# Rotating 96 planes by a quarter turn: two groups of four slabs in place of one, with two quarters laid out in rows by ScalarE

## The chip, the cores and the metric

One Trainium2 chip, one core. The metric is the device time of one launch in microseconds (us), a median over runs. Of the engines, VectorE (DVE in the profile) does the transposes, ScalarE (ACT) does plain copies, SyncE (SP) issues every DMA. TensorE does nothing; GpSimd (POOL) sets four constants at the start.

## The reference

```python
# x: float32, 32 x 3 x 256 x 256
return np.rot90(x, k=-1, axes=(-2, -1)).astype(np.float32)
```

Each of the 96 planes of 256 x 256 floats is turned clockwise: element (h, w) goes to row w, column 255 - h. No arithmetic is done. 25.17 MB are read and 25.17 MB written.

## The kernel before

**Slabs and groups.** A slab is 128 x 16 rows of 256 floats: 2 MB, or 4096 floats (16 KB) on each of the 128 partitions. There are 12 slabs, and all of them stay in SBUF at once, in five tiles `u0` to `u4` of `sizes = (2, 2, 2, 4, 2)` slabs. Each group is turned in place, so the store of a group reads the tile that its load filled.

**Loads.** A partition gets runs of neighbouring rows, and the length of one run is the length of one DMA row: 8 KB in group 0 (lines 55 and 56), 16 KB in the groups of two slabs and 32 KB in the group of four (line 66). SP issues all loads in order, group by group, 2 MB or 1 MB each; the very last 2 MB are split in two halves of 1 MB (lines 63 and 64), the first of which is called `mark`.

**Turning.** VectorE's transpose works on blocks of 32 x 32: it swaps 32 partitions with 32 elements of its free axis. Which 32 elements form a block is chosen by the access pattern, so one transpose instruction over 128 x 2048 elements moves a quarter of two slabs. The 16 rows x 16 columns of small blocks on a partition are cut in four quarters by the low and high half of the column index c and of the row index r. The changed kernel names them A = (low c, low r), B = (high, low), C = (high, high) and D = (low, high). Turned, each quarter lands where another one was: D's goes to A's old place, and so on round the cycle. So `turn_group` first takes A out into a spare tile (line 88, `held`), then turns D, C and B within the group (line 93), each into the place that the one before has left, and lastly ScalarE copies the held quarter into the place that B has left (line 98). A group of two slabs has one such cycle (T = 1), a group of four has two (T = 2), which alternate: the data of `t` = 0 lands in the places of `t` = 1 and the other way round. Group 0 has its own form, `turn_slab` (lines 72 and 78), which needs only one slab in order to start.

The source of each of these transposes is read in the order `c r g a`: the innermost step (a) is half the group's tile, the next (g) is 16 elements or 64 bytes. No two elements read one after the other are neighbours. The spare tiles are `spare0` and `spare1`, 8 KB per partition each, which fill PSUM, and `extra`, 8 KB in SBUF.

**Stores.** Two per group, 2 MB or 4 MB, always in rows of 16 KB (lines 106 and 113), issued by SP after all the loads. The first store waits for `mark`, so it is issued while the last 1 MB of loads is still on its way. The store of a group waits for VectorE and ScalarE to have finished it.

Of the kernel before, what the change touches and what calls it, by code (L numbers as in the profile page):

```python
# [1 line left out]

# [4 lines left out]


@with_exitstack  # L10
def kernel(
    ctx: ExitStack,
    tc: tile.TileContext,
    x: bass.AP,
    out: bass.AP,
):

    nc = tc.nc
    fp32 = mybir.dt.float32

    B, C, H, W = x.shape
    P = nc.NUM_PARTITIONS
    R = 16  # L30
    E = R * W
    hw = R // 2
    low, high = slice(0, hw), slice(hw, R)

    rows_in = x.rearrange("b c h w -> (b c h) w")
    rows_out = out.rearrange("b c h w -> (b c h) w")

    sizes = (2, 2, 2, 4, 2)
    first = [sum(sizes[:n]) for n in range(len(sizes))]
    groups = [  # L40
        ctx.enter_context(tc.tile_pool(name=f"group{n}", bufs=1)).tile([P, s, E], fp32, name=f"u{n}")
        for n, s in enumerate(sizes)
    ]
    psum = ctx.enter_context(tc.tile_pool(name="psum", bufs=1, space=bass.MemoryType.PSUM))
    spare = [psum.tile([P, E // 2], fp32, name=f"spare{h}") for h in range(2)]
    extra = ctx.enter_context(tc.tile_pool(name="extra", bufs=1)).tile([P, E // 2], fp32, name="extra")

    def rows_of(rows, n):
        return rows[first[n] * P * R : (first[n] + sizes[n]) * P * R]


    ld = rows_of(rows_in, 0).rearrange("(s i p r) w -> s i p (r w)", s=2, i=2, p=P)
    home = [groups[0][:, s].rearrange("p (i f) -> p i f", i=2) for s in range(2)]
    for i in range(2):
        nc.sync.dma_start(out=home[0][:, i], in_=ld[1, i])  # L55
    nc.sync.dma_start(out=home[1], in_=ld[0].transpose([1, 0, 2]))
    for n in range(1, len(sizes)):
        I = sizes[n]
        ld = rows_of(rows_in, n).rearrange("(a i m r) w -> i m a (r w)", a=2, i=I, m=P // I)
        to = groups[n].rearrange("p s f -> p (s f)").rearrange("p (a f) -> p a f", a=2)  # L60
        for i in range(I):
            if (n, i) == (len(sizes) - 1, I - 1):
                mark = nc.sync.dma_start(out=to[i::I, 0], in_=ld[i][:, 0])
                nc.sync.dma_start(out=to[i::I, 1], in_=ld[i][:, 1])
            else:
                nc.sync.dma_start(out=to[i::I], in_=ld[i])

    def turn_slab(src, dsts):
        s = src.rearrange("p (i r g c) -> p c r g i", i=2, r=R // 2, c=R)
        for h, d in enumerate(dsts):  # L70
            d = d.rearrange("p (c k r) -> p c r k", c=hw, r=R // 2)[:, :, ::-1, ::-1]
            nc.vector.transpose(out=d, in_=s[:, h * hw : (h + 1) * hw])  # L72

    u = groups[0]
    turn_slab(u[:, 0], spare)
    turn_slab(u[:, 1], [u[:, 0, : E // 2], u[:, 0, E // 2 :]])
    for h in range(2):
        nc.scalar.copy(out=u[:, 1, h * E // 2 : (h + 1) * E // 2], in_=spare[h])  # L78

    def turn_group(n, held):  # L80
        I = sizes[n]
        T = I // 2
        K = W // (R * T)
        u = groups[n].rearrange("p s f -> p (s f)")
        src = u.rearrange("p (a t r g c) -> p t c r g a", a=2, t=T, r=R, c=R)
        dst = u.rearrange("p (i c k t r) -> p t c r k i", i=I, c=R, k=K, t=T)[:, ::-1, :, ::-1, ::-1, :]
        for t in range(T):
            nc.vector.transpose(  # L88
                out=held[t].rearrange("p (i c k r) -> p c r k i", i=I, c=hw, k=K)[:, :, ::-1, ::-1, :],
                in_=src[:, t, low, low])  # L90
        for c, r in ((low, high), (high, high), (high, low)):
            for t in range(T):
                nc.vector.transpose(out=dst[:, t, c, r], in_=src[:, t, c, r])  # L93
        back = u.rearrange("p (i c k t r) -> p t i c k r", i=I, c=R, k=K, t=T)[:, ::-1]
        for t in range(T):
            kept = held[t].rearrange("p (i c k r) -> p i c k r", i=I, c=hw, k=K)
            for i in range(I):
                nc.scalar.copy(out=back[:, t, i, low, :, high], in_=kept[:, i])  # L98

    for n, held in enumerate(([extra], [spare[1]], spare, [extra]), 1):  # L100
        turn_group(n, held)


    st = rows_of(rows_out, 0).rearrange("(s i m r) w -> i m s (r w)", s=2, i=2, m=P // 2)
    for a in range(2):
        put = nc.sync.dma_start(out=st[a], in_=groups[0][a::2])
        if a == 0:
            tc.add_manual_dep(put.ins, mark.ins.name, mybir.DependencyInfo(
                mybir.DependencyClass.Sync, mybir.DependencyReason.SCHED_ONLY), reason="stores after loads")
    for n in range(1, len(sizes)):  # L110
        st = rows_of(rows_out, n).rearrange("(a i m r) w -> a m i (r w)", a=2, i=sizes[n], m=P // 2)
        for a in range(2):
            nc.sync.dma_start(out=st[a], in_=groups[n][a::2])


# [1 line left out]
_INS = ['x']  # L117
_OUTS = [((32, 3, 256, 256), 'float32')]


# [23 lines left out]
```

## Time and profile before

| | |
|---|---|
| median of 3 runs | 122.94 us (122.88 to 123.08) |
| the profiled execution's own time | 122.88 us |
| its span, first to last instruction | 121.1 us |
| outside the span | 1.78 us |
| VectorE busy | 87.4 us, 24 transposes |
| ScalarE busy | 14.9 us, 16 copies and one table load |
| DMA | 50.33 MB, 3456 packets, 97.6% of the 16 engines' span |

The profile is of one execution. A DMA packet here is one row of a transfer on one of the 16 DMA engines; 384 of the 3456 packets are the 4-byte completion marks, 16 for each of the 24 DMAs. A strip of 40 digits shows how busy an engine was in each fortieth of the span, in tenths; the GB/s strip below it counts a packet's bytes where it starts. A DMA's time "to landing" runs from its issue by SP to its last byte's arrival.

### The profile page before, as it was taken

To read this page: it belongs to the slowest core of one execution; us is meant where nothing else is said; L and a number is where in the kernel's file an instruction comes from. 1 tells how busy PE (TensorE), PEld (TensorE's weight loads), DVE (VectorE), ACT (ScalarE), POOL (GpSimd) and SP (SyncE) were. 2 spreads that over 40 slices of the span, in tenths; PEclk is the share of its full clock that TensorE was granted. 3 is DMA by queue.
4 is the path that set the end of the run, shared out by engine and by line. 5 is a ranking of instruction groups with operands and counts; after the bars stand their busy time and mean duration, and the time that the engine had idled before them with its cause. 6 is when DMAs were issued, how large, how long until landed. Compare 5 with 4: busy or idle time off the path is not lost.

```text
span 121.1 us, 131 instructions
## 1 busy us (share of the span) xinstructions
DVE 87.4 (72%) x24; ACT 14.9 (12%) x17; POOL 0.2 (0%) x4
## 2 busy tenths in 40 slices
DVE  0039999999999999999999999999999600000000
ACT  0000400380005100060000000318000330000000
POOL 0000000000000000000000000000000000000000
DMA  2999999999989898999999999999999999999994
GB/s 89 428 428 422 452 433 433 433 433 433 520 346 520 346 520 346 428 422 411 433 433 428 433 433 428 417 417 433 428 433 433 433 433 433 433 433 433 433 422 184
DMA packets 3456, 50.33 MB, mean 416 GB/s; under 512 B 384, under 2 KB 384, under 8 KB 384
## 3 DMA queue, kind: packets, MB, share of 16 engines
q1 hardware_dynamic: 3456, 50.33, 97.6%
HBM read 25.17 MB, written 25.17 MB: 416 GB/s over the span
## 4 chain that ended last, share of the span: by engine, by line
DVE 66%; issue 6%; DMA 6%; ACT 1%; ACTq 1%; SPq 0%; DVEq 0%
DVE u L93 39%; DVE spare L88 9%; DVE extra L88 6%; DVE u L72 6%; DVE spare L72 6%; DMA u<-in_x_dram 6%; ACT u L98 1%; ACTq L139 1%; SPq L55 0%; DVEq L88 0%; DVEq L72 0%
## 5 line engine op out<-in xcount | busy, mean ns | idle before, releaser
L93 DVE STREAM_TRANSPOSE u<-u 128x2048 f32<-128x2048 f32 x15 | 54.4, 3649 | 0.4
L72 DVE STREAM_TRANSPOSE spare<-u 128x2048 f32<-128x2048 f32 x2 | 7.1, 3586 | 8.1 <-DMA u<-in_x_dram 8.1
L98 ACT COPY u<-spare 128x512 f32<-128x512 f32 (+1 forms) x10 | 6.0, 687 | 38.5 <-DVE u L93 38.5
L88 DVE STREAM_TRANSPOSE spare<-u 128x2048 f32<-128x2048 f32 x3 | 10.7, 3588 | 0.0
L72 DVE STREAM_TRANSPOSE u<-u 128x2048 f32<-128x2048 f32 x2 | 7.8, 3988 | 0.0
L88 DVE STREAM_TRANSPOSE extra<-u 128x2048 f32<-128x2048 f32 x2 | 7.8, 3896 | 0.0
L98 ACT COPY u<-extra 128x1024 f32<-128x1024 f32 x4 | 4.0, 1043 | 22.8 <-DVE u L93 22.8
L78 ACT COPY u<-spare 128x2048 f32<-128x2048 f32 x2 | 3.6, 1870 | 8.7 <-DVE u L72 8.7
L78 ACT ACT_TABLE_LOAD x1 | 1.3, 1283 | 13.0 <-DMA u<-in_x_dram 13.0
L128 POOL MEMSET const-uint8-127<- 128x1 uint8 x1 | 0.1, 103 | 0.0
L128 POOL MEMSET const-bfloat16-1.0<- 128x1 bf16 x1 | 0.1, 102 | 0.0
L128 POOL MEMSET const-float32-0.0<- 128x1 f32 x1 | 0.1, 99 | 0.2 <-issue 0.2
L128 POOL MEMSET const-float32-1.0<- 128x1 f32 x1 | 0.1, 99 | 0.0
## 6 DMA issues: line engine op xcount, KB each, us to landing
u<-in_x_dram SPq DMA_DIRECT2D x10, 2048.0 KB, 30.4
out_dram<-u SPq DMA_DIRECT2D x8, 2048.0 KB, 18.2
out_dram<-u SPq DMA_DIRECT2D x2, 4096.0 KB, 21.1
u<-in_x_dram SPq DMA_DIRECT2D x4, 1024.0 KB, 20.5
```

The lines of the kernel that those rows point to most:

```text
L72: nc.vector.transpose(out=d, in_=s[:, h * hw : (h + 1) * hw])
L78: nc.scalar.copy(out=u[:, 1, h * E // 2 : (h + 1) * E // 2], in_=spare[h])
L88: nc.vector.transpose(out=held[t].rearrange("p (i c k r) -> p c r k i", i=I, c=hw, k=K)[:, :, ::-1, ::-1, :], in_=src[:, t, low, low])
L93: nc.vector.transpose(out=dst[:, t, c, r], in_=src[:, t, c, r])
L98: nc.scalar.copy(out=back[:, t, i, low, :, high], in_=kept[:, i])
L128: nc = _bacc.Bacc("TRN2", target_bir_lowering=False, num_devices=1)
L139: with _tile.TileContext(nc) as tc:
```

## The change

The groups become `sizes = (2, 2, 4, 4)`. Loads of the first two have rows of 16 KB, those of the last two 32 KB. Group 0 is treated like the others; its first 2 MB are split in two DMAs. There are still 14 loads; the stores are 8 in place of 10, the last four of 4 MB.

Groups 0 and 1 (two slabs) are turned as before, `turn_pair`: A to a PSUM tile, then D, C, B in place, then two ScalarE copies.

In group 2 ScalarE copies quarter A of `t` = 0 into `extra` in the order in which the transpose reads (`line`), VectorE turns `extra` in place in plain order (`extra<-extra`), and a ScalarE copy scatters the result to its place (`unline`). Quarter D of `t` = 0 goes the same way through `spare1`, which is PSUM. The other six quarters are turned as before.

In group 3 ScalarE copies quarter A of `t` = 0, unturned, into `spare1` (in two halves, in runs of 8 elements), from where the last transpose turns it into its place. Quarter A of `t` = 1 is turned into two tiles: seven eighths into a new SBUF tile `most`, one eighth into the first 256 elements of `spare0`.

VectorE has 25 transposes in place of 24: 22 as before in kind and size, the two in plain order, and A of group 3 in two pieces. ScalarE has 19 copies in place of 16. The order of instructions on these two engines is fixed by `keep`, an ordering that adds no wait.

```diff
-    sizes = (2, 2, 2, 4, 2)
+    sizes = (2, 2, 4, 4)
...
-            if (n, i) == (len(sizes) - 1, I - 1):
+            if (n, i) in ((0, 0), (len(sizes) - 1, I - 1)):
                 mark = nc.sync.dma_start(out=to[i::I, 0], in_=ld[i][:, 0])
                 nc.sync.dma_start(out=to[i::I, 1], in_=ld[i][:, 1])
             else:
                 nc.sync.dma_start(out=to[i::I], in_=ld[i])
...
+        def leave(self, t, held, c=low, n=hw):
+            kept = held.rearrange("p (i c k r) -> p c r k i", i=self.I, c=n, k=self.K)
+            turn(out=kept[:, :, ::-1, ::-1, :], in_=self.src[:, t, c, low])
+        def enter(self, t, held, i, c=low, n=hw):
+            kept = held.rearrange("p (i c k r) -> p i c k r", i=self.I, c=n, k=self.K)
+            copy(out=self.back[:, t, i, c, :, high], in_=kept[:, i])
+        def move(self, t, c, r):
+            turn(out=self.dst[:, t, c, r], in_=self.src[:, t, c, r])
+        def line(self, t, c, r, row):
+            row = row.rearrange("p (c r g a) -> p c r g a", c=hw, r=hw, a=2)
+            copy(out=row, in_=self.src[:, t, c, r])
+        def unline(self, t, c, r, row):
+            row = row.rearrange("p (c r k i) -> p c r k i", c=hw, r=hw, k=self.K)
+            copy(out=self.dst[:, t, c, r], in_=row)
...
+    turn_pair(g0, spare[0])
+    for i in range(2):
+        g0.enter(0, spare[0], i)
+    turn_pair(g1, spare[1])
+    g2.line(0, *A, extra)
+    g2.leave(1, spare[0])
+    for i in range(2):
+        g1.enter(0, spare[1], i)
+    turn(out=extra, in_=extra)
+    g2.line(0, *D, spare[1])
+    g2.move(1, *D)
+    turn(out=spare[1], in_=spare[1])
+    g2.unline(0, *D, spare[1])
+    for q in (C_, B_):
+        for t in range(2):
+            g2.move(t, *q)
+    kept = spare[1].rearrange("p (a r g c) -> p a r g c", a=2, r=hw, c=hw)
+    for a in range(2):
+        copy(out=kept[:, a], in_=g3.raw[:, 0, a, low, :, low])
+    for i in (0, 2, 1, 3):
+        g2.enter(1, spare[0], i)
+    rest = spare[0][:, : Q // hw]
+    g3.leave(1, most, slice(0, cut), cut)
+    g3.leave(1, rest, slice(cut, hw), 1)
+    g2.unline(0, *A, extra)
+    for q in (D, C_, B_):
+        for t in range(2):
+            g3.move(t, *q)
+    for i in (0, 2, 1, 3):
+        g3.enter(1, most, i, slice(0, cut), cut)
+    held = rest.rearrange("p (i k r) -> p i k r", i=4, k=g3.K)
+    copy(out=g3.back[:, 1, :, cut, :, high], in_=held)
+    turn(out=g3.dst[:, 0, low, low], in_=kept.rearrange("p a r g c -> p c r g a"))
```

## The prediction

> **What bounds the kernel now.** I read the busy strips first, because they show at once which resource has no gap.
>
> ```profile
> DVE  0039999999999999999999999999999600000000
> ACT  0000400380005100060000000318000330000000
> ...
> DMA  2999999999989898999999999999999999999994
> GB/s 89 428 428 422 452 433 433 433 433 433 520 346 520 346 520 346 428 422 411 433 433 428 433 433 428 417 417 433 428 433 433 433 433 433 433 433 433 433 422 184
> ```
>
> The DMA strip is full from the second slice to the last but one (the 8s and the 520/346 pairs are 32 KB packets counted where they start). VectorE ends at about 96 us, four fifths through, and the queue still has 25 us of stores to write. So the DMA queue sets the end, although the page's chain of waits names VectorE: that chain follows engines back from the last instruction and doesn't show that stores were standing in line. Only two things can move the time: the time that a byte takes in the queue, and a gap in it.
>
> What a byte takes, by row length, comes from the SP timeline and the windows. Each late load waits for an earlier one to land, so its issue marks that landing.
>
> ```profile
> 7.98 0.60 SPq L66 DMA_DIRECT2D u<-in_x_dram  x1
> 12.95 0.60 SPq L66 DMA_DIRECT2D u<-in_x_dram  x1
> 17.84 0.61 SPq L66 DMA_DIRECT2D u<-in_x_dram  x1
> 22.75 0.51 SPq L63 DMA_DIRECT2D u<-in_x_dram  x1
> 27.64 0.49 SPq L64 DMA_DIRECT2D u<-in_x_dram  x1
> ```
>
> ```profile
> 3.00:12.00 9.00, 3.94 (x2) 0.00 (x0) 0.00 (x0) 1.00 1.02 429
> 13.00:31.00 18.00, 17.90 (x6) 4.92 (x3) 0.00 (x0) 1.00 1.01 429
> 33.00:50.00 17.00, 16.86 (x6) 1.99 (x2) 0.00 (x0) 1.00 1.01 434
> ```
>
> Between two such marks lie 2 MB. Rows of 8 KB: 12.95 - 7.98 = 4.97 us. Rows of 16 KB: (27.64 - 12.95) / 3 = 4.90 us. Rows of 32 KB: the load issued at 4.22 has 28.3 us to landing (32.5), the one issued at 12.95 has 39.0 (51.9), and four loads lie between: 4.85 us. The windows (last two columns: DMA share, GB/s) agree that only the 32 KB stretch is faster.
>
> **The DMA side of the change.** Group 0's 4 MB go from 8 to 16 KB rows: 2 x (4.97 - 4.90) = 0.14 us less. Before, 8 MB in 32 KB rows; after, 16 MB. Four 2 MB pieces go from 4.90 to 4.85: 0.20 us less, the rounding leaving 0.15 to 0.20. Two fewer stores save 32 of the 4-byte packets over 16 engines, nothing I can read. Sum: 0.3 us, so loads end at 61.4 instead of 61.7 (the last one, issued at 27.64, has 34.1 us to landing). Stores have the same rows and bytes: 120.3 - 61.7 = 58.5 us both times. One cost stands against it: the first load's issue took 0.38 us (8 KB rows, line 55), while a 1 MB load of 16 KB rows takes 0.51 (line 63). If the first byte waits for that, 0.13 us is lost; the range is 0 to 0.13 and I take 0.
>
> The Trainium skill ("DMA: Bandwidth & Descriptors", section "Why small descriptors are slow (HBM only)") gives a fixed cost of about three cycles per packet and says that joining is "only worth it at ≤256 B desc size"; by it rows of 8, 16 and 32 KB are alike, this part brings nothing and the time stays 122.9. The marks above show 4.97, 4.90 and 4.85, and I go by them.
>
> **Is the queue still fed?** Each group's stores must be issued before the stores ahead have run out. The last group is now 8 MB, not 4, so its deadline moves forward by 10 us: the queue runs out of groups 0 to 2 at 61.4 + 16.8 MB of stores. Before, the same 16.8 MB ended at 84.25 + 16.5 = 100.7 (landing of the first 4 MB store), 39.0 us after the loads: after, 100.4. And VectorE starts later: group 0 now needs its whole 4 MB (12.8 us, 0.14 earlier than the 12.95 above) where it needed 2 MB (8.06). So I sum VectorE's work.
>
> ```profile
> 8.06 7.08 DVE L72 STREAM_TRANSPOSE spare<-u 128x2048 f32<-128x2048 f32 x2 [8.06 <-DMA u<-in_x_dram]
> ...
> 37.60 3.59 DVE L88 STREAM_TRANSPOSE spare<-u 128x2048 f32<-128x2048 f32 x1
> 37.74 1.99 ACT L98 COPY u<-extra 128x1024 f32<-128x1024 f32 x2 [11.07 <-DVE u L93]
> 41.23 10.93 DVE L93 STREAM_TRANSPOSE u<-u 128x2048 f32<-128x2048 f32 x3
> 52.12 7.08 DVE L88 STREAM_TRANSPOSE spare<-u 128x2048 f32<-128x2048 f32 x2
> ...
> 59.23 21.92 DVE L93 STREAM_TRANSPOSE u<-u 128x2048 f32<-128x2048 f32 x6
> ...
> 81.04 3.88 DVE L88 STREAM_TRANSPOSE extra<-u 128x2048 f32<-128x2048 f32 x1
> ...
> 95.92 1.99 ACT L98 COPY u<-extra 128x1024 f32<-128x1024 f32 x2 [11.70 <-DVE u L93]
> ```
>
> The transposes stand back to back, 3.5 to 3.9 us each.
> - Groups 0 and 1: a two-slab group took 52.12 - 37.60 = 14.52. Start at 12.8 + 0.1 (the wait's release), so 12.9 + 29.0 = 41.9. Group 2's data lands at 12.8 + 2 x 4.90 + 4 x 4.85 = 42.0; VectorE goes on at 42.1, a wait of 0.2.
> - Group 2: A of t = 1 (3.6), five moves (21.9 less one of 3.5 = 18.4), and the two in plain order, x each. Nothing in the trace reads or writes in order on VectorE. The lower end is ScalarE's plain 128x2048 copy, 1.87 us (L78); the upper is 3.6 to 3.9, the transposes in column order. All forms of these cost nearly the same, to PSUM or SBUF, slab or group; what they share is that neighbours are read far apart, which the plain ones drop. The copy is the only row of a 2048-element run, so I take it plus the 0.33 by which like transposes differ (3.57 to 3.90): 2.2. Sum 22.0 + 4.4 = 26.4.
> - Group 3: A of t = 1 in two pieces: 7/8 of 3.9 (the SBUF row, extra<-u) = 3.4, and 1/8 with its own start, 0.6; six moves 21.9; the last transpose reads PSUM in jumps, bounds 2.2 to 3.9, nearest the column-order rows: 3.6. Sum 29.5.
> - End: 42.1 + 26.4 + 29.5 = 98.0, plus 0.2 for the wait below: 98.2. The store is issued there; ScalarE's last copies (4 x 0.55 and 0.4, after the sixth move at 94.6) end at about 96 and lie beside it.
>
> The Trainium skill ("Vector Engine (DVE) Microarchitecture Reference", section "5.2 Measured stream behaviour on trn2 (trn3 not measured)") gives 1.054 ns per column for runs of two or more adjacent words and 1.73 for a source that hops at every element; by it a plain transpose is 2.2 us, and the sum is as above.
>
> **ScalarE's new copies.** `line` of A starts when group 2 lands (42.0) and VectorE wants it at 45.7, after its own first transpose. Bounds: 1.87 us in order, and 3.6 if ScalarE pays for jumps as VectorE's rows do; I take 3.6, being the row with the same read pattern: ready at about 45.9, a wait of 0.2. Behind it in ScalarE's order stand group 1's two copies (2.0; its stores aren't due before 71) and `line` of D, ready by 51.5; VectorE wants that at 45.9 + 2.2 + 3.9 = 52.0. `unline` of D is behind that and must only be done before group 2's stores. The four copies that empty `spare0` end at 70, and VectorE needs it for the eighth at 72; `unline` of A then ends by 73.6. Group 2's stores are due at 80.9 minus the start-up: covered by 5 us.
>
> The same section speaks against the change here: if the hop costs ScalarE what it costs a VectorE port, `line` is 3.5 us and not 1.9, and VectorE's wait appears; the sum holds that already.
>
> **The margin.** How much ahead must a store be issued? The first load was issued at 0.73; the first slice (3.03 us) moved 89 GB/s, which at 428 is 0.63 us, so flow began at 2.4: 1.7 after issue. The first store was issued 2.3 us before the last load landed (59.43 and 61.7), and the strip shows no gap there. So the lead needed lies between 0 and 2.3; I take 1.7. Deadline 100.4 - 1.7 = 98.7, issue at 98.2: half a microsecond in hand. That is thin, and it decides the sign.
>
> **Sum.** On time: 122.88 - 0.3 = 122.6 for the profiled execution, which is 0.06 below the median of its runs; against the median also 122.6 (122.64). With the first issue's 0.13 it is 122.75. A difference of 0.2% (0.25 us, 122.69) is about what a measurement of this kernel can tell from no change.
>
> **Rivals.**
> 1. *In order is no cheaper* (slower). Two transposes at 3.6 in place of 2.2 put the last store at 98.2 + 2.8 = 101.0. The queue stands dry for 101.0 + 1.7 - 100.4 = 2.3 us: 124.9; with a lead of 1.0, 124.2. For it: every transpose in the trace costs 3.5 or more. Against: none of them reads in order. It decides from x = 2.5 on.
> 2. *ScalarE's jumping copies are slow* (slower). With `line` taking L, VectorE waits L - 3.6 at `extra` and then another L - 4.2 at `spare1`. At L = 4.7 that is 1.6, and 123.5. For it: no ScalarE row reads in jumps. Against: its copies that write in runs of 8 cost no more than plain ones (1.01 against 0.94 for half of 1.87). It decides from L = 4.2.
> 3. *Small lateness*: the terms add up to 0.5 to 1.2 us more than I have, or the lead is 2.3. 122.7 to 123.5.
> 4. *The first issue takes 0.13*: the queue is fed, but half of the gain goes at the start: 122.75, no change.
>
> **How the numbers follow.** On time 0.62 (of it 0.47 over 0.2% faster, 0.15 within, by rival 4 and the rounding of the 0.3), rival 1 0.15, rival 2 0.10, rival 3 0.13 (0.03 of it within 0.2%). Faster 0.47, same 0.18, slower 0.35. The forecast alone is 122.45 to 122.8. The range 122.4 to 124.0 leaves out most of rival 1 and the ends.
>
> **What would show it.** Right: DMA strip without a gap, loads ended at 61.4, plain transposes at 2.2, the last transpose ended near 98, the first of the last two stores issued before 98.7. Wrong: a slice below 9 near 100 us, VectorE waiting for ScalarE at 46 or 52, or plain transposes above 2.5.

## The result, and the profile after

The changed kernel is slower by 0.7%: 123.78 us median (123.72 to 124.24, 6 runs) against 123.02 (122.88 to 123.14, 6 runs), a ratio of 1.0068 (95% interval 1.0052 to 1.0085). The profiled execution took 123.72 us with a span of 121.9, against 122.88 and 121.1. (Beside the two transposes in plain order and the two pieces of A, its 25 have 21 others, not 22.)

The busy strips and the DMA totals of the changed kernel:

```profile
DVE  0000699999999999999999999999999960000000
ACT  0000400006000099928363194000003400000000
...
DMA  3999999998979897979899999999999989999994
GB/s 86 387 430 435 441 435 435 446 505 355 516 344 516 344 516 344 516 344 516 344 430 430 430 430 430 425 425 430 430 430 430 430 355 430 430 430 430 430 430 172
DMA packets 2912, 50.33 MB, mean 413 GB/s; under 512 B 352, under 2 KB 352, under 8 KB 352
```

Two places differ from before beyond the way that 32 KB packets are counted. The second slice moves 387 GB/s (428 before): the queue starts late. And the 33rd slice, 97.5 to 100.6 us, has an 8 in the DMA strip and 355 GB/s: a hole, late enough that the queue was waiting for VectorE, whose strip now ends in that same slice.

VectorE and ScalarE from the landing of group 2 on, and the last two stores, by the timeline (start, duration, engine, line, operation, count):

```profile
42.49 4.24 ACT L75 COPY extra<-u 128x2048 f32<-128x2048 f32 x1 [12.58 <-DMA u<-in_x_dram]
42.55 4.22 DVE L72 STREAM_TRANSPOSE spare<-u 128x2048 f32<-128x2048 f32 x1 [0.17 <-DMA u<-in_x_dram]
46.63 1.90 ACT L75 COPY u<-spare 128x1024 f32<-128x1024 f32 x2
46.76 2.31 DVE L72 STREAM_TRANSPOSE extra<-extra 128x2048 f32<-128x2048 f32 x1
48.56 4.01 ACT L75 COPY spare<-u 128x2048 f32<-128x2048 f32 x1
48.99 4.03 DVE L72 STREAM_TRANSPOSE u<-u 128x2048 f32<-128x2048 f32 x1
52.75 2.47 DVE L72 STREAM_TRANSPOSE spare<-spare 128x2048 f32<-128x2048 f32 x1
54.99 14.82 DVE L72 STREAM_TRANSPOSE u<-u 128x2048 f32<-128x2048 f32 x4
55.26 3.88 ACT L75 COPY u<-spare 128x2048 f32<-128x2048 f32 x1 [2.67 <-DVE spare L72]
...
69.72 3.60 DVE L72 STREAM_TRANSPOSE most<-u 128x1792 f32<-128x1792 f32 x1
...
73.73 22.16 DVE L72 STREAM_TRANSPOSE u<-u 128x2048 f32<-128x2048 f32 x6
...
95.92 3.60 DVE L72 STREAM_TRANSPOSE u<-spare 128x2048 f32<-128x2048 f32 x1
...
99.60 1.26 SPq L158 DMA_DIRECT2D out_dram<-u  x2
```

The transposes in plain order take 2.31 and 2.47 us. But the column-order transpose that runs beside ScalarE's first `line` takes 4.22 (3.6 before), and that copy itself 4.24. VectorE ends at 99.5 and the store is issued at 99.60; forecast were 98.0 and 98.2. The store ahead of it, issued at 75.21, has 25.9 us to landing, so the queue would be empty at 101.1: the new store came 1.5 us before that.

From the landings of the two profiled executions, where the 0.85 us between their spans (121.09 and 121.94) lies:

| piece | before | after | difference |
|---|---|---|---|
| first 1 MB landed | 5.49 | 5.90 | +0.41 |
| from there to the last load | 56.25 | 56.01 | -0.24 |
| hole before the last two stores | 0 | 0.38 | +0.38 |
| the rest of the stores | 58.54 | 58.71 | +0.17 |
| from the last landing to the end of the span | 0.81 | 0.94 | +0.13 |

The hole is the time between the landings of the store ahead (101.1) and of the late one (111.3, issued at 99.60 with 11.7 to landing) less the 9.8 us that 4 MB take without a hole. So the loads do bring most of the 0.3 that was forecast, and two costs of 0.4 and two smaller ones outweigh it. The experiments took the two large ones apart. The last row is SP's: at the end it waits for the stores one after the other in a fixed order, and a wait takes 0.06 us even when its store has long landed. Before, the last store stands last in that order; in the changed kernel two waits come behind it.

### The profile page after: what moved, and what is told of

It is laid out like the page before. It is cut to its first block, busy times and chain, and to the rows that moved or that the text cites. A ratio compares the mean times of both kernels' runs of the same rounds, so it can differ in the third digit from the quotient of the medians.

```text
span 121.9 us, 132 instructions
## 1 busy us (share of the span) xinstructions
DVE 85.6 (70%) x25; ACT 27.3 (22%) x20; POOL 0.2 (0%) x4
## 4 chain that ended last, share of the span: by engine, by line
DVE 44%; DMA 30%; SPq 4%; issue 3%; DVEq 0%
DVE u L72 33%; DMA u<-in_x_dram 30%; DVE spare L72 6%; SPq L59 3%; DVE most L72 3%; DVE extra L72 2%; SPq L56 0%; SPq L57 0%; DVEq L72 0%
## 5 line engine op out<-in xcount | busy, mean ns | idle before, releaser
L72 DVE STREAM_TRANSPOSE spare<-u 128x2048 f32<-128x2048 f32 (+1 forms) x4 | 11.9, 2979 | 13.6 <-DMA u<-in_x_dram 13.6
L75 ACT COPY u<-spare 128x1024 f32<-128x1024 f32 (+3 forms) x10 | 10.2, 1062 | 20.7 <-DVE u L72 18.0
L75 ACT COPY extra<-u 128x2048 f32<-128x2048 f32 x1 | 4.2, 4235 | 12.6 <-DMA u<-in_x_dram 12.6
L75 ACT COPY spare<-u 128x1024 f32<-128x1024 f32 (+1 forms) x3 | 6.0, 2016 | 2.9 <-DMA u<-in_x_dram 2.9
L75 ACT COPY u<-most 128x448 f32<-128x448 f32 x4 | 2.1, 564 | 20.3 <-DVE u L72 20.3
L75 ACT ACT_TABLE_LOAD x1 | 1.3, 1283 | 13.3 <-DMA u<-in_x_dram 13.3
L75 ACT COPY u<-extra 128x2048 f32<-128x2048 f32 x1 | 3.7, 3739 | 0.0
L72 DVE STREAM_TRANSPOSE u<-spare 128x2048 f32<-128x2048 f32 x1 | 3.6, 3605 | 0.0
L72 DVE STREAM_TRANSPOSE most<-u 128x1792 f32<-128x1792 f32 x1 | 3.6, 3603 | 0.0
L72 DVE STREAM_TRANSPOSE spare<-spare 128x2048 f32<-128x2048 f32 x1 | 2.5, 2474 | 0.0
L72 DVE STREAM_TRANSPOSE extra<-extra 128x2048 f32<-128x2048 f32 x1 | 2.3, 2311 | 0.0
```

The lines of the kernel that those rows point to most:

```text
L72: keep(nc.vector.transpose(out=out, in_=in_))
L75: keep(nc.scalar.copy(out=out, in_=in_))
```

## The experiments

All times are medians of five runs or more, beside runs of the kernel before on the same chip (122.97 to 123.03), unless said.

**1. Group 0 taken back.**

```diff
+    ld = rows_in[: sizes[0] * P * R].rearrange("(s i p r) w -> s i p (r w)", s=2, i=2, p=P)
+    for i in range(2):
+        nc.sync.dma_start(out=home[0][:, i], in_=ld[1, i])
+    nc.sync.dma_start(out=home[1], in_=ld[0].transpose([1, 0, 2]))
...
-    turn_pair(g0, spare[0])
...
+    turn_slab(v[:, 0], spare)
+    turn_slab(v[:, 1], [v[:, 0, : E // 2], v[:, 0, E // 2 :]])
+    turn_pair(g1, extra)
...
-    turn_pair(g1, spare[1])
...
```

> The changed kernel with group 0 as in the kernel before: its loads in rows of 8 KB, its slab form on VectorE, all else as changed (group 1's quarter A is held in extra). Theory: half of the loss is at the start, because a first DMA of 64 rows of 16 KB is issued in 0.60 us (0.38 before) and its first byte moves at 2.11 us (1.74 before). Then the first bytes move at 1.74 again, loads end at 61.6 us (61.9 changed, 61.7 before), group 2 lands at 42.2 instead of 42.5, VectorE still ends near 99.2 because group 2's landing sets it (it is idle from 37.4 to 42.2), the gap in the queue near 101 us stays at 0.4 us, and the time is 123.3. Rival: the start costs nothing that lasts and all of the loss is the late last store: 123.7 to 123.8.

123.60 us, ratio 1.0044 (1.0031 to 1.0057). The first byte moves at 1.74 again, but the first MB landed at 5.7, between the two, so in this execution the loads ended only 0.1 us sooner. VectorE had idle time before group 2 and gained next to nothing at its end; the last but one store was issued at 99.52, 1.2 us before the queue was empty (100.7), and the hole grew to 0.7 us, where 0.4 was expected; the 123.3 was missed too. That the queue was empty 0.4 us sooner than in the changed kernel comes only to 0.1 from the loads. The other 0.3 is the stores ahead, which ran faster in this execution, for a reason that stays open. What the queue gains ahead of a late store, the hole eats.

**2. No last transpose.**

```diff
-    turn(out=g3.dst[:, 0, low, low], in_=kept.rearrange("p a r g c -> p c r g a"))
```

> The changed kernel without its last transpose (quarter A of t = 0 of group 3 isn't put in place). Theory: the queue runs dry for 0.4 us near 101 us because the first of the last two stores is issued at 99.6, 1.5 us before the queue is empty. Without the transpose it is issued at 97.3, there is no gap, and the time falls by 0.4 to 123.3; loads still end at 61.9. Rival: the 4 MB stores or the end of the queue cost it whatever the issue time: 123.7 to 123.8.

123.49 us, ratio 1.0035 (1.0022 to 1.0047). The store is issued at 97.22, 4.0 us ahead, and the windows show no hole (last two columns: DMA share, GB/s; first the changed kernel, then this one):

```profile
98.00:101.00 3.00, 1.52 (x1) 0.00 (x0) 0.00 (x0) 1.00 0.90 382
101.00:104.00 3.00, 0.00 (x0) 0.00 (x0) 0.00 (x0) 1.00 0.91 382
```

```profile
98.00:101.00 3.00, 0.00 (x0) 0.00 (x0) 0.00 (x0) 1.00 1.05 437
101.00:104.00 3.00, 0.00 (x0) 0.00 (x0) 0.00 (x0) 1.00 1.02 437
```

So the hole is the late store. The median fell by 0.29 us, not 0.4. The profiled execution, the slowest of the five at 123.54, had its first MB landed at 6.1, later than any other of this form; whether the other four started late isn't on record.

**3. Group 2 in column order, no help from ScalarE.**

```diff
-    g2.line(0, *A, extra)
+    g2.leave(0, extra)
     g2.leave(1, spare[0])
...
-    turn(out=extra, in_=extra)
-    g2.line(0, *D, spare[1])
-    g2.move(1, *D)
-    turn(out=spare[1], in_=spare[1])
-    g2.unline(0, *D, spare[1])
-    for q in (C_, B_):
+    for q in (D, C_, B_):
         for t in range(2):
             g2.move(t, *q)
...
-    g2.unline(0, *A, extra)
+    for i in (0, 2, 1, 3):
+        g2.enter(0, extra, i)
```

> The changed kernel with group 2 turned as before the change: no ScalarE line or unline, eight transposes in column order (quarter A of t = 0 held in extra). By the prediction's terms (two plain transposes at 2.2 for 3.6, nothing else) VectorE would end 2.8 us later than 99.5, and the time would be 126.5. Theory now: ScalarE's jumping copies slow VectorE's transposes beside them by about 1.9 us in sum, so the two plain transposes gain only 0.8 us net: VectorE ends at 100.3 to 100.5, the gap near 101 grows from 0.4 to about 1.2, and the time is 124.6.

125.55 us, ratio 1.0203 (1.0189 to 1.0216): 1.8 us slower than the changed kernel. My expectation of 124.6 was wrong; I had held the interference for larger than it is. VectorE in this kernel from the landing of group 2 on, and its last two stores:

```profile
42.48 4.08 DVE L72 STREAM_TRANSPOSE extra<-u 128x2048 f32<-128x2048 f32 x1
46.40 3.54 DVE L72 STREAM_TRANSPOSE spare<-u 128x2048 f32<-128x2048 f32 x1
49.97 21.95 DVE L72 STREAM_TRANSPOSE u<-u 128x2048 f32<-128x2048 f32 x6
71.55 3.82 DVE L72 STREAM_TRANSPOSE most<-u 128x1792 f32<-128x1792 f32 x1
74.95 0.79 DVE L72 STREAM_TRANSPOSE spare<-u 128x256 f32<-128x256 f32 x1
75.78 21.95 DVE L72 STREAM_TRANSPOSE u<-u 128x2048 f32<-128x2048 f32 x6
97.76 3.61 DVE L72 STREAM_TRANSPOSE u<-spare 128x2048 f32<-128x2048 f32 x1
...
101.45 1.26 SPq L154 DMA_DIRECT2D out_dram<-u  x2
```

Group 2 takes 71.55 - 42.48 = 29.1 us here and 69.72 - 42.55 = 27.2 in the changed kernel. ScalarE's help is worth 1.9 us, where the sum had 2.8. The store is issued at 101.45, after the queue has run dry (101.1), and the hole is 2.2 us.

**4. The same copies, straight.**

```diff
-    g2.line(0, *A, extra)
+    flat = groups[2].rearrange("p s f -> p (s f)")
+    copy(out=extra, in_=flat[:, :Q])
...
-    g2.line(0, *D, spare[1])
+    copy(out=spare[1], in_=flat[:, Q : 2 * Q])
...
-    g2.unline(0, *D, spare[1])
+    copy(out=most, in_=spare[1][:, : Q // hw * cut])
...
-    g2.unline(0, *A, extra)
+    copy(out=extra, in_=extra)
```

> The changed kernel with ScalarE's four big copies made straight: line reads 2048 elements in one run of the same tile of group 2, unline writes in one run to a spare tile (1792 elements for quarter D). This leaves out the laying out, so two quarters of group 2 are not turned; VectorE's instructions are all the same. Theory: the transposes of 4.0 to 4.2 us beside ScalarE's copies are slow because both engines jump through SBUF at once. Then line takes 1.9 us instead of 4.2, the five transposes that took 4.22, 4.03, 4.02, 3.60 (seven eighths) and 3.89 take about 3.6, 3.6 to 3.9, 3.6, 3.4 and 3.6, VectorE ends at 98.0, the gap near 101 is gone and the time is 123.3. Rival: they are slow through the 32 KB rows or the places they write, whatever ScalarE does: 4.0 to 4.2 us stay and the time is 123.7.

123.47 us, ratio 1.0038 (1.0025 to 1.0050).

```profile
42.63 1.90 ACT L75 COPY extra<-u 128x2048 f32<-128x2048 f32 x1 [12.59 <-DMA u<-in_x_dram]
42.69 3.73 DVE L72 STREAM_TRANSPOSE spare<-u 128x2048 f32<-128x2048 f32 x1
...
46.39 1.87 ACT L75 COPY spare<-u 128x2048 f32<-128x2048 f32 x1
48.43 3.95 DVE L72 STREAM_TRANSPOSE u<-u 128x2048 f32<-128x2048 f32 x1
...
54.38 7.17 DVE L72 STREAM_TRANSPOSE u<-u 128x2048 f32<-128x2048 f32 x2
...
72.83 21.93 DVE L72 STREAM_TRANSPOSE u<-u 128x2048 f32<-128x2048 f32 x6
...
98.48 1.65 SPq L159 DMA_DIRECT2D out_dram<-u  x2
```

The same transposes, on the same places, beside copies of the same size (the one of quarter D in one eighth less): the first falls from 4.22 to 3.73, the pair C from 7.44 to 7.17, the six of group 3 from 22.16 to 21.93. D of t = 1 hardly moves (4.03 to 3.95) and takes 3.9 without any copy beside it (experiment 3), so that one is its place. From group 2's start to VectorE's end it is 55.7 us in place of 57.0. The store is issued at 98.48, 2.7 us ahead, and the hole is gone. The theory holds in direction, with 1.25 us in sum. From start to next start, 0.66 of it is at the first transpose (4.21 to 3.55), 0.28 at the pair C and 0.24 in group 3. Each kernel has one trace here: in the six traces that keep the copies and the last transpose, the same stretch takes 56.8 to 57.5 us.

Three things stay open. Straight copies are also shorter, and the two that stand in for `unline` write to other tiles, so jumps, tile and length aren't told apart. Nor does it say which of the two engines' jumps, reading or writing, is the worse. And the 0.66 can be read in two ways. VectorE's waits in the changed kernel are a single line, the two waits for loads:

```profile
DVE spare L72 <- DMA u<-in_x_dram: 13.6, 2, 13.4
```

By it the transpose itself was slow. But in all seven traces with these copies the turn of `extra` starts within 0.04 us of the end of `line` and of that transpose alike. So a transpose of 3.6 would have had to wait for `line`, and the same time would have gone.

**5. The kernel before, profiled again.**

> The kernel before, profiled once more, for how far one execution of it differs from another: the first MB landed at 5.49 us and the loads ended at 61.74 in the execution shown. With group 0 taken back, the same first loads landed at 5.72. If that spread is the machine's, this one lands between 5.5 and 5.75 and its loads end between 61.7 and 62.0; if it is the kernel's, it lands at 5.5 again.

123.11 us in its one run. Its first MB landed at 5.7 and its loads ended at 62.0; the stores took 58.5 us as before. So the start varies by 0.2 us from one execution to the next. The form before landed at 5.5 to 5.7 in five executions (three of them in experiments 1, 9 and 10), the changed form at 5.9 to 6.1 in five, so the 0.4 of the table above is a fair middle of 0.2 to 0.6.

**6. The first MB in rows of 8 KB.**

```diff
-            if (n, i) in ((0, 0), (len(sizes) - 1, I - 1)):
+            if (n, i) == (0, 0):
+                for h in range(2):
+                    cols = slice(h * Q, (h + 1) * Q)
+                    nc.sync.dma_start(out=to[i::I, :, cols], in_=ld[i][:, :, cols])
+            elif (n, i) == (len(sizes) - 1, I - 1):
```

> The changed kernel with the first two loads of 1 MB cut by columns, 64 partitions x 2 rows of 8 KB, where they were 64 rows of 16 KB; all else as changed. Theory: the row length of the first DMA delays the first byte. Then its issue takes 0.4 us, the first byte moves at 1.75, the first MB lands at 5.5 to 5.7 (5.90 changed), loads end at 61.6 to 61.7; the gap near 101 stays at 0.4 because VectorE and the queue are shifted alike; 123.5. Rival: it is the 64 partitions in steps of two, not the row length: issue 0.6, first byte 2.1, 123.75.

124.11 us, ratio 1.0095 (1.0079 to 1.0112): worse than the changed kernel. The theory fell: with shorter rows the first issue took 0.74 us, the first byte moved at 2.27 and the first MB landed at 6.2. Row length is not what delays the start. (The pair C beside `unline` also took longer here, 4.56 and 4.40 against 4.02 and 3.86. So the store was issued at 100.38, 1.0 us before the queue was empty, and the hole was 0.9 us.)

**7. The kernel before with a first DMA in steps of two.** This is the clean test of what is left: the same bytes, the same 8 KB rows, only the partitions differ.

```diff
-    for i in range(2):
-        nc.sync.dma_start(out=home[0][:, i], in_=ld[1, i])
+    for e in range(2):
+        nc.sync.dma_start(out=home[0][e::2], in_=ld[1][:, e::2].transpose([1, 0, 2]))
```

> The kernel before with one edit: its first two loads of 1 MB, both in rows of 8 KB, take 64 partitions in steps of two (both halves of their 16 KB) where they took 128 partitions in steps of one. The same bytes and row length. Theory: the form of the first DMA, not its row length, delays the start: its issue takes 0.74 us in place of 0.38, the first byte moves at 2.27, the first MB lands at 6.1 to 6.2, loads end at 62.3, and with VectorE far ahead of the stores the whole delay is seen: 122.97 + 0.45 = 123.4. Rival: the late start in the changed kernel comes from something else: first byte 1.75 to 1.8 and 123.0.

123.53 us, ratio 1.0042 (1.0030 to 1.0055), 0.50 us more than the kernel before. The SP timeline and the windows of the first microseconds, of the kernel before and then of this one:

```profile
0.73 0.85 SPq L55 DMA_DIRECT2D u<-in_x_dram  x2
```

```profile
1.70:2.10 0.40, 0.00 (x0) 0.00 (x0) 0.00 (x0) 1.00 0.60 82
2.10:2.70 0.60, 0.00 (x0) 0.00 (x0) 0.00 (x0) 1.00 0.44 164
```

```profile
0.73 1.42 SPq L55 DMA_DIRECT2D u<-in_x_dram  x2
```

```profile
1.70:2.10 0.40, 0.00 (x0) 0.00 (x0) 0.00 (x0) 1.00 0.00 0
2.10:2.70 0.60, 0.00 (x0) 0.00 (x0) 0.00 (x0) 1.00 1.07 137
```

Two issues take 1.42 us in place of 0.85, and nothing moves before 2.1. The form of the very first DMAs is the start's price. Whether it is the step of two, the 64 partitions or the two runs on each isn't told apart by this.

**8. Half a store early.** The last transpose writes only the lower eight of a slab's 16 rows.

```diff
-    turn(out=g3.dst[:, 0, low, low], in_=kept.rearrange("p a r g c -> p c r g a"))
...
+        if n == 3:
...
+            nc.sync.dma_start(out=half[0][:, :2, high], in_=u3[0::2, :2, high])
+            turn(out=g3.dst[:, 0, low, low], in_=kept.rearrange("p a r g c -> p c r g a"))
+            nc.sync.dma_start(out=half[0][:, :2, low], in_=u3[0::2, :2, low])
+            nc.sync.dma_start(out=st[0][:, 2:], in_=groups[3][0::2, 2:])
+            nc.sync.dma_start(out=st[1], in_=groups[3][1::2])
+            continue
```

> The changed kernel with the upper eight of the 16 rows of two slabs of group 3 stored (64 partitions x 2 x 8 KB, 1 MB) before the last transpose, which writes only lower rows; the rest of the first store follows after it in two DMAs. Theory: the queue needs its next DMA issued 1.9 us before it runs out. This one is issued at 96.0 and covers 2.4 us, the rest comes at 99.6, 3.9 us ahead: no gap, 2 MB in 8 KB rows cost 0.05, so 123.4. Rival: the gap belongs to the group of 4 MB stores and stays: 123.8.

123.44 us, ratio 1.0037 (1.0024 to 1.0051): 0.34 less than the changed kernel.

```profile
96.32 0.60 SPq L159 DMA_DIRECT2D out_dram<-u  x1
99.99 0.60 SPq L161 DMA_DIRECT2D out_dram<-u  x1
```

VectorE ended even later than in the changed kernel (99.9), and it no longer mattered: 1 MB issued at 96.3 carried the queue over. The gain is not the hole's 0.38 alone: in its trace the stores took 58.9 us (58.7 in the changed kernel, less its hole), and with ten stores again the end after the last landing is back at 0.81.

**9. Both repairs.** Group 0 as in experiment 1 and the early half of experiment 8.

> Both repairs: group 0 as in the kernel before (its 8 KB rows and slab form) and the early store of 1 MB of group 3. Theory: the gap of 0.70 us of the kernel with group 0 alone goes, 0.05 us is paid for the shorter rows: 123.60 - 0.65 = 122.95, the time of the kernel before within what can be told. If the 32 KB rows are worth the 0.15 us that the loads after group 0 show, it is at 122.85 or so. Rival: taking away the gap brings up another wait: 123.3 or more.

122.96 us (11 runs), ratio 0.9999 (0.9991 to 1.0008). The strip has neither the late start nor the hole (by the landings the last 8 MB take 19.7 us, where two stores of 4 MB without a hole take 19.6):

```profile
DMA  4999999998989898989899999999999999999994
GB/s 92 427 427 424 446 432 432 432 519 346 519 346 519 346 519 346 519 346 519 346 432 432 432 427 432 432 427 432 432 432 432 432 389 413 419 432 432 427 432 178
```

From the changed kernel, the early half takes away 0.34 us (123.78 to 123.44) and group 0's old form another 0.48 (to 122.96); the change had cost 0.76. The gain of the rows does not show: loads ended at 61.6, 0.15 before those of the kernel before, but the stores took longer, 58.9 us against 58.5.

**10. Smaller stores.** Experiment 9 with its 4 MB stores in two of 2 MB.

```diff
+            for j in (0, 2):
+                nc.sync.dma_start(out=st[1][:, j : j + 2], in_=groups[3][1::2, j : j + 2])
...
+        if n == 2:
+            for a in range(2):
+                for j in (0, 2):
+                    nc.sync.dma_start(out=st[a][:, j : j + 2], in_=groups[2][a::2, j : j + 2])
```

> The kernel with both repairs (group 0 of before and the early store) and its 4 MB stores cut into 2 MB ones. Where no gap is, 4 MB stores took 9.79 to 9.84 us each and 2 MB stores 4.83 to 4.90, so the cut may win 0.05 us on each of three: 122.96 - 0.15 = 122.8, under the kernel before for the first time. Rival: the pace belongs to the execution, not to the size: 122.95.

123.21 us (11 runs), ratio 1.0014 (1.0004 to 1.0024), no gain. In its trace the stores took 58.6 us against 58.9 in experiment 9, and yet the runs were slower. The expectation failed. Part of it is the end: 0.98 us from the last landing (120.39) to the end of the span, against 0.81 in experiment 9, because three of SP's waits come behind the last store's. That is 0.17 of the 0.25 us between the medians; the rest has no cause on record. No kernel here beat the one before.

## Why the prediction was wrong, step by step

**Right.** The queue sets the end; the hole near 100 us and the thin margin that decides the sign were both named, and half a microsecond was indeed too little. The rows of 32 KB brought 0.15 us between group 0's landing and the last load: 48.80 us in all three traces with the grouping of before, 48.64 to 48.67 in all nine with the changed one. Plain transposes took 2.31 and 2.47 against 2.2. The last transpose, put at 3.6, took 3.60; the eighth 0.52 against 0.6.

The Trainium skill ("Vector Engine (DVE) Microarchitecture Reference", section 5.2) gave 1.054 ns per column for neighbours, measured with another operation, an estimate of 2.2 us, and 2.31 us is near it. By "DMA: Bandwidth & Descriptors", section "Why small descriptors are slow (HBM only)", joining is only worth it up to 256 B, so longer rows should bring next to nothing; the landings show the 0.15.

**The margin, half a microsecond, was lost in two terms.** The step that failed is "Is the queue still fed?".
- *VectorE's end.* Each transpose was taken at its duration before, as if ScalarE's new copies lay beside it for nothing. Beside the copies as they are, VectorE took 1.25 us more than beside straight ones (experiment 4). Half of that has the size of rival 2: `line` took 4.24, past the point of 4.2, so L - 3.6 is 0.64, and 0.66 was lost at that place. The profile books it as a slower transpose and not as a wait, and the two aren't told apart there. The other half, in the pair C and in group 3, lies in transposes that wait for no copy; no rival had it. The bound of 3.6 for `line` was too low as well. (The 0.2 of wait in the sum does not follow from its own terms: 42.0 + 3.6 is 45.6, before the 45.7 at which VectorE wants the data.) The start, 0.5 later than summed (group 0's data was there at 13.3, not 12.8), moved VectorE and the deadline alike, so it did not open the hole.
- *The lead.* I took 1.7 us within 0 to 2.3. Four kernels had a hole, and lead and hole add up to the same in each, because the late store landed 11.7 us after its issue each time, 1.9 more than the 9.8 of a store without a hole:

| | issued | queue empty | lead | hole | sum |
|---|---|---|---|---|---|
| changed kernel | 99.60 | 101.1 | 1.5 | 0.4 | 1.9 |
| experiment 1 | 99.52 | 100.7 | 1.2 | 0.7 | 1.9 |
| experiment 3 | 101.45 | 101.1 | -0.3 | 2.2 | 1.9 |
| experiment 6 | 100.38 | 101.4 | 1.0 | 0.9 | 1.9 |

With 2.7 and 4.0 us of lead (experiments 4 and 2) there was none. Here a store of 4 MB had to be issued 1.9 us before the queue was empty.

**The start.** This step failed too: "the range is 0 to 0.13 and I take 0" was wrong in size and in cause. I compared two issues by row length; the first issue took 0.60 us (a late one of the same form 0.51), the first byte moved at 2.11 and not 1.74, and the first MB landed some 0.4 later. Experiments 6 and 7 show that it's the DMA's form. This alone takes the forecast gain away (0.41 against the 0.24 that the loads won after it), and with the hole and the longer end gives the sign.

So rival 3, small lateness, names the mechanism: the store was issued 1.4 us later than summed, the queue was empty 0.7 later, and the lead was 0.2 longer, which turns half a microsecond in hand into a hole of 0.4. Its 122.7 to 123.5 leaves out the 123.78; the first issue, rival 4, came in addition. I had taken them as exclusive; they added up.

**Stores.** Forecast the same, 58.5 us. The grouping of before needed 58.5 in all three traces; the changed grouping, less its hole, 58.4 to 58.9 in nine, five of them at 58.7 to 58.8. Of what the extra 0.2 us consists stays open: 2 MB stores did not settle it. Two fewer stores were put at nothing; the order of SP's last waits, which changed with them, cost 0.13.

The same section 5.2 of the microarchitecture page states that the scalar engine and VectorE, run together on disjoint tiles, each keep their full rate. Here both worked in one tile, in jumps, a case that it does not state: `line` and the transpose beside it took 4.24 and 4.22, against 1.90 and 3.73 with straight copies. How much of the 4.24 is ScalarE's own jumping isn't known, as no run has such a copy alone.

## What to carry to other kernels

When a queue sets the end, a change that makes the last piece larger moves its deadline forward by the transfer time of what was added (here from 110.5 to 101.1 us); sum up the engine's end against that deadline and add the lead (1.9 us here), before counting any gain. Work moved to an idle engine was not free for the engine it helped: price the helped engine's own instructions beside the helper. Where the last piece can't be ready sooner, store the part of it that is ready: 1 MB early closed the hole.

## What the runs showed of the hardware

- A ScalarE copy of 128x2048 that reads in the order of the transposes, no two neighbours in a row, took 3.65 to 4.24 us beside VectorE's work, and 1.87 to 1.90 when it read straight through. One that scatters its output took 3.71 to 4.42. Beside them VectorE's column-order transposes went from 3.6 to as much as 4.2, in experiments 6 and 8 to 4.3 to 4.6.
- The issue of the first DMA and the time to its first byte depend on its form: 0.38 us and 1.74 for 128 partitions in steps of one, 0.73 and 2.25 for 64 in steps of two with two runs of 8 KB on each. Half a microsecond of the whole time hung on it.
- The first MB of one and the same kernel landed at 5.5 and at 5.7 us in two executions.
- The program ended 0.81 us after the last landing where SP's last wait was for the store that landed last, and 0.94 where two waits for stores long landed came behind it.
